# Attention scores as full-height matrix products: high and low query halves stacked in the array's rows

## The chip, the cores and the metric

One core of one Trainium2 chip runs the whole kernel. The metric is device time in microseconds (us), the median of several executions. TensorE (PE) multiplies matrices; its weight loads are a row of their own in the profile (PEld). VectorE (DVE), ScalarE (ACT) and GpSimd (POOL) do element-wise work, each in the order in which its instructions were written; SyncE (SP) starts transfers.

## The reference, cut to what matters

One layer of causal attention with a linear position penalty, 256 tokens, width 1024, 16 heads of 64. The sequence is one block long, so the block selection falls away.

```
h = rms_norm(x, norm_g)                       # 256 x 1024
q, k, v, gate = split(h @ w_in, 4)            # w_in 1024 x 4096
s = q_h @ k_h.T / 8 - slope_h * (t_q - t_k)   # per head, t_k <= t_q
o_h = softmax(s) @ v_h
out = rms_norm(x + (o * silu(gate)) @ w_out, final_g)
```

## The kernel before

Every product is made to nearly full float32 precision from pieces in the format fp32r: an operand is split into a high part (a copy that is rounded to fp32r, made by ACT) and a low part (the rest, a subtraction, made by DVE). A product is then high x high, plus high x low, plus low x high: three matmuls.

The weights arrive in 40 pieces of 128 x 1024 numbers. Each is split by `split_hi` (ACT, the copies of line 118) and `split_lo` (DVE, line 252); four pieces can be split ahead of their use. The projections run in the order of `PARTS`: v 0, q 0, k 0, g 0, q 1, k 1, g 1, q 2, k 2, q 3, k 3, v 1, g 2, g 3. A part of q, k or g gives four heads, that is two pairs of heads; `j` counts the parts and `p` the pairs. The output projection follows, with the 8 pairs as its 8 steps, and the last steps (pairs 4 to 7) stand at its end. The final norm and the stores come after it.

When a part of q or k is done, `fiber_evac` scales it into a tile `z` (DVE, line 512), copies it to the high part (ACT, line 118), and subtracts (DVE, line 524). The two heads of a pair lie in the two halves of the 128 partitions. `scores` then multiplies them for two pairs (four heads) at once, four times in the kernel: each matmul uses the 64 rows of one head, and the two heads of a pair stand next to each other in the program and use different halves of the array. There are 20 such matmuls in a block (line 354). For queries 128 to 255 (`m` = 1) there are three products per head; for queries 0 to 127 (`m` = 0) there are two, of which the first computes high and low keys side by side, and DVE adds these two parts later (line 387). `fiber_pair` makes the softmax: score plus bias with its minimum (lines 387 and 390), exponential (ACT), reciprocal (line 400), normalisation (line 410 on DVE or a copy on ACT, line 407 to 411), transposes (line 111), split of the probabilities (ACT and line 434), product with v, the gate (lines 468 to 474) and the split of the result into `oh` (ACT) and `ol` (line 479).

The order on each engine is written out by the program itself: `Plan` keeps a clock for PE, ACT, DVE and POOL with a cost for each instruction, and "fibers" (one for each evacuation and each pair) are woken when PE's clock passes the time at which their operands should be there. `at_q` and `at_k` hold the time at which a pair's operands are ready; `scores` wakes at the latest of them. `fill` places weight splits when their due time comes near. A normalisation goes to ACT if the plan has ACT more than 800 ns behind DVE's clock, otherwise to DVE:

```
if plan.t["act"] + NORM < plan.t["dve"]:
    d = max(d, act(o, o, AF.Copy, c1 - c0, d_ri, False, scale=ri[:, cc:cc + 1]))
else:
    nc.vector.tensor_scalar(o, o, ri[:, cc:cc + 1], None, op0=ALU.mult)
```

`SWITCH` is a cost of 100 ns that the plan adds before and after a score block. At the start POOL makes 16 bias tiles (`make_bias`, line 221), then the two powers of the norm (line 566).

Of the kernel before, what the change touches and what calls it, by code (L numbers as in the profile page):

```python
# [13 lines left out]
P = 128  # L14
# [43 lines left out]
COLD = 6800.0  # L58
WARM_END = 9000.0
NL = 4  # L60
SWITCH = 100.0


class Plan:
# [18 lines left out]
def f32(ap):  # L83
    return ap.bitcast(F32)
# [3 lines left out]
def trunk(ctx: ExitStack, tc, laid, fin_g, out):  # L88
# [7 lines left out]
    sp = ctx.enter_context(tc.tile_pool(name="sp", bufs=NPR))  # L96
    ptp = ctx.enter_context(tc.tile_pool(name="ptp", bufs=NPT))
    qp = ctx.enter_context(tc.tile_pool(name="qp", bufs=NKB))
    khp = ctx.enter_context(tc.tile_pool(name="khp", bufs=NKB))
    zp = ctx.enter_context(tc.tile_pool(name="zp", bufs=2))  # L100
    csp = ctx.enter_context(tc.tile_pool(name="csp", bufs=2))
    ogp = ctx.enter_context(tc.tile_pool(name="ogp", bufs=2))
# [112 lines left out]
    rows = const.tile([P, S], F32, name="rows")  # L215
    rows8 = const.tile([P, S], F32, name="rows8")
    rowsh = const.tile([P, S], F32, name="rowsh")

    def make_bias(h):
        slope = -(2.0 ** (-8.0 * (h + 1) / H))  # L220
# [104 lines left out]
    def scores(p):  # L325


        while not all(u in at_k and u in at_q for u in (p, p + 1)):
            yield poll()
        yield max(t[u] for t in (at_k, at_q) for u in (p, p + 1))  # L330
        while stage["s"] < p:
            yield poll()
        while True:
            b0 = take(keep[0] + 3)
            if b0 is not None:
                break
            yield poll()
        both = [b0] + [take_now() for _ in range(3)]
        plan.pe += SWITCH
        for u in (p, p + 1):  # L340
            of_pair[u] = both[2 * (u - p):2 * (u - p) + 2], {}
        for m, c in ((1, slice(0, S)), (0, slice(S, S + P))):
            for u in (p, p + 1):
                bs, at_s = of_pair[u]
                (qh, ql), kt = (qs[u][:, 0], qs[u][:, 1]), ks[u]
                n = c.stop - c.start

                terms = ((qh, (0, 1)), (ql, (0,))) if m == 0 else ((qh, (0,)), (qh, (1,)), (ql, (0,)))
                for jj, (q, ts) in enumerate(terms):
                    for a in range(2):  # L350
                        rr = slice(a * DH, (a + 1) * DH)
                        o = bs[a]["t"][:, c.start:c.start + n * len(ts)]
                        o = o.rearrange("p (t n) -> p t n", n=n)
                        nc.tensor.matmul(o, q[rr, m * P:(m + 1) * P], kt[rr, ts[0]:ts[-1] + 1, 0:n],  # L354
                                         start=jj == 0, stop=jj == len(terms) - 1, skip_group_check=True)
                    at_s[m] = plan.mm(n * len(ts))
        plan.pe += SWITCH
        stage["s"] = p + 2
        yield 0

# [127 lines left out]
    def fiber_evac(kind, j, f, b, r):  # L488
        ps = b["t"]
        if kind == "v":  # L490
            hs = slice(j * H // 2, (j + 1) * H // 2)
            ps = ps.rearrange("p (h n) -> p h n", n=DH)
            while not rstd_at:
                yield poll()
            yield max(r, rstd_at[-1]) - 200
            e = act(vv[f][:, hs, 0, :], ps, AF.Copy, CW, max(r, rstd_at[-1]), True, scale=rstd[f])
            yield e - 200
            nc.vector.scalar_tensor_tensor(vv[f][:, hs, 1, :], ps, rstd[f], f32(vv[f][:, hs, 0, :]), op0=ALU.mult, op1=ALU.subtract)
            d = dve(CW, e, extra=62)
            give(b, d)  # L500
            at_v[j] = max(d, at_v.get(j, 0))
            nv[j] += 1
            return
        while not have_rows:
            yield poll()
        yield max(r, have_rows[0]) - 200

        pairs = slice(2 * j, 2 * j + 2)
        ps = ps.rearrange("p (f n) -> p f n", f=2)
        z = zp.tile([P, 2, S], F32, name="z")  # L510
        rb = {"q": rows8, "k": rows, "g": rowsh}[kind].unsqueeze(1).to_broadcast([P, 2, S])
        nc.vector.tensor_mul(z, ps, rb)
        d = dve(2 * S, max(r, have_rows[0]))
        give(b, d)
        if kind != "g":
            while stage["s"] < 2 * (j - NKB + 1):
                yield poll()
        yield d - 100
        if kind != "g":
            pool = qp if kind == "q" else khp  # L520
            both = pool.tile([P, 2, 2, S], F32R, name=kind)
            e = act(both[:, 0], z, AF.Copy, 2 * S, d, False)
            yield e - 100
            nc.vector.tensor_sub(both[:, 1], z, f32(both[:, 0]))
            d = dve(2 * S, e)
            for a in range(2):
                (qs if kind == "q" else ks)[2 * j + a] = both[:, :, a]
                (at_q if kind == "q" else at_k)[2 * j + a] = d
        else:
            e = act(sg[:, pairs, :], z, AF.Tanh, 2 * S, d, False)  # L530
            yield e - 100
            nc.vector.scalar_tensor_tensor(sg[:, pairs, :], sg[:, pairs, :], 1.0, z, op0=ALU.add, op1=ALU.mult)
            d = dve(2 * S, e)
            at_g[2 * j] = at_g[2 * j + 1] = d

    with tc.manual_schedule():
# [48 lines left out]

        for h in range(H):
            make_bias(h)
        warm_to(3480.0)
        acc = banks[4:6]
        for b in acc:  # L590
# [231 lines left out]
```

## Time and profile before

| | |
|---|---|
| median of 3 runs | 143.28 us (143.06 to 143.43) |
| the profiled execution | 143.68 us |
| its span in the trace | 141.9 us |
| mean granted TensorE clock in the span | 0.994 of full speed |
| PE busy | 135.1 us, 95% |
| DVE busy | 122.9 us, 87% |
| ACT busy | 94.4 us, 67% |
| POOL busy | 13.8 us, 10% |

The span is the part of the execution between the first and the last instruction; 1.78 us lie around it. Busy time is the time in which an engine runs at least one instruction. Two consecutive instructions of one engine overlap in part, so the distance between two starts, and not the duration of one, says how much of the engine's time an instruction takes.

### The profile page before, as it was taken

The page shows a single profiled execution, that of the slowest core. Times are in us where ns is not written, and L with a number is a line of the kernel's source. Part 1 is how long each engine was busy: PE and PEld are TensorE (multiplying, and loading weights), DVE is VectorE, ACT ScalarE, POOL GpSimd, SP SyncE. Part 2 cuts the span into 40 slices and gives each one's busy share as a digit, 9 for nine tenths or more (in the row PEclk, how much of TensorE's full clock was granted, in tenths as well). Part 3 has the DMA queues.
Part 4 walks back from the last instruction along what each step waited for, and adds up shares of the span by engine and source line. Part 5 has one row for each costly group of instructions (what it writes and reads, how often), then busy time and mean ns, then how long its engine had stood idle before and what let it go on. Part 6 is the DMA issues. An engine that isn't in the chain of part 4 may idle for free.

```text
span 141.9 us, 2687 instructions
## 1 busy us (share of the span) xinstructions
PE 135.1 (95%) x977; PEld 124.6 (88%) x977; DVE 122.9 (87%) x286; ACT 94.4 (67%) x198; POOL 13.8 (10%) x29
## 2 busy tenths in 40 slices
PE   7999999999999999999999999999999999999930
PEld 5688899999999999999999997778999988888830
DVE  0989579988989999989989999997999999994970
ACT  3498989665878674877772993769959755812340
POOL 7992130000000000000000000000000000000210
PEclk9999999999999999999999999999999999999997
DMA  4999998788204734244445704675055735000034
GB/s 166 321 396 406 404 393 292 241 260 281 106 0 148 216 113 158 109 145 155 159 141 170 258 18 148 200 247 151 0 172 177 245 118 182 0 0 0 0 148 150
DMA packets 8077, 24.81 MB, mean 175 GB/s; under 512 B 896, under 2 KB 1280, under 8 KB 8064
## 3 DMA queue, kind: packets, MB, share of 16 engines
q1 hardware_dynamic: 7632, 23.73, 48.3%
q10 hardware_dynamic: 432, 0.92, 1.7%
q8 instruction: 7, 0.11, 0.3%
q14 instruction: 6, 0.05, 0.1%
HBM read 23.60 MB, written 1.05 MB: 174 GB/s over the span
## 4 chain that ended last, share of the span: by engine, by line
PE 91%; issue 3%; DVE 2%; POOL 1%; ACT 1%; POOLq 1%
PE bank L107 81%; PE bank L111 4%; PE bank L354 4%; PE bank L543 2%; DVE x L756 1%; POOL fr L770 1%; DVE bias L760 1%; ACT bias L777 1%; POOLq L818 1%; DVE bias L765 0%; DVE oh L208 0%; DVE fms L732 0%; DVE eps_t L212 0%; DVE fms L760 0%
## 5 line engine op out<-in xcount | busy, mean ns | idle before, releaser
L107 PE MATMUL bank<-xl,whi 128*128 128x256 f32 x192 | 55.2, 288 | 0.0
L107 PE MATMUL bank<-xh,wlo 128*128 128x256 f32 x192 | 55.0, 287 | 0.0
L107 PE MATMUL bank<-xh,whi 128*128 128x256 f32 x192 | 55.0, 287 | 0.0
L252 DVE TENSOR_TENSOR wlo<-w,whi 128x1024 fp32r<-128x1024 f32 (+1 forms) x43 | 48.6, 1136 | 4.6 <-ACT whi L118 4.5
L118 ACT ACTIVATE whi<-w 128x1024 fp32r<-128x1024 f32 (+1 forms) x43 | 41.5, 976 | 13.2 <-PE bank L107 5.9
L107 PEld LDWEIGHTS bank<-xl,whi 128*128 128x128 f32 x192 | 36.2, 188 | 0.2
L107 PEld LDWEIGHTS bank<-xh,whi 128*128 128x128 f32 x192 | 36.2, 188 | 0.2
L107 PEld LDWEIGHTS bank<-xh,wlo 128*128 128x128 f32 x192 | 36.2, 188 | 0.0
L118 ACT ACTIVATE pr<-st,mx 128x256 f32<-128x256 f32 (+1 forms) x32 | 14.2, 447 | 1.8 <-DVE mx L390 1.6
L770 POOL TENSOR_TENSOR fr<-fms,mhalf 128x1 f32<-128x1 f32 x2 | 1.6, 799 | 114.7 <-DVE fms L760 114.7
L107 PE MATMUL bank<-whi,oh 128*128 128x512 f32 (+1 forms) x35 | 12.3, 352 | 0.0
L107 PE MATMUL bank<-wlo,oh 128*128 128x512 f32 (+1 forms) x35 | 12.3, 351 | 0.0
L107 PE MATMUL bank<-whi,ol 128*128 128x512 f32 (+1 forms) x35 | 12.3, 351 | 0.0
L107 PE MATMUL bank<-whi,xh 128*128 128x512 f32 x32 | 12.3, 425 | 0.0
L111 PE MATMUL bank<-ident,pr 128*128 128x128 f32 x48 | 12.0, 272 | 0.0
L107 PE MATMUL bank<-whi,xl 128*128 128x512 f32 x32 | 11.9, 415 | 0.0
L107 PE MATMUL bank<-wlo,xh 128*128 128x512 f32 x32 | 11.9, 414 | 0.0
L118 ACT ACTIVATE pt<-bank 128x384 fp32r<-128x384 f32 x16 | 7.8, 489 | 3.2 <-PE bank L111 3.1
L107 PE MATMUL bank<-pt,vv 128*128 128x256 f32 x48 | 9.8, 281 | 0.0
L434 DVE TENSOR_TENSOR pt<-bank,pt 128x384 fp32r<-128x384 f32 x16 | 8.7, 551 | 0.7 <-ACT pt L118 0.6
L221 POOL TENSOR_SCALAR bias<-dist 128x256 f32<-128x256 f32 x16 | 8.8, 551 | 1.0
L107 PEld LDWEIGHTS bank<-pt,vv 128*128 128x128 f32 x48 | 8.1, 189 | 0.2
(80 smaller groups left out, 195.4 us busy)
## 6 DMA issues: line engine op xcount, KB each, us to landing
w<-in_laid SPq DMA_DIRECT2D x36, 512.0 KB, 3.5
w<-in_laid SPq DMA_DIRECT2D x7, 256.0 KB, 5.5
x<-in_laid SPq DMA_DIRECT2D x2, 512.0 KB, 6.9
head<-in_laid SPq DMA_DIRECT2D x3, 256.0 KB, 5.7
gf<-in_fin_g ACTq DMA_DIRECT2D x1, 512.0 KB, 5.5
out<-bias SPq DMA_DIRECT2D x2, 256.0 KB, 2.0
out<-bias SPq DMA_DIRECT2D x1, 320.0 KB, 2.3
w<-in_laid ACTq DMA_DIRECT2D x1, 256.0 KB, 2.9
```

The lines of the kernel that those rows point to most:

```text
L107: nc.tensor.matmul(o, a, b, start=start, stop=stop, skip_group_check=True)
L111: nc.tensor.transpose(o, a, ident)
L118: nc.scalar.activation(o, i, fn, scale=scale, **kw)
L221: nc.gpsimd.tensor_scalar(bias[:, h, :], dist, slope, 0.0, op0=ALU.mult, op1=ALU.add)
L252: nc.vector.tensor_sub(wlo[i][:, c], w32[i][:, c], f32(whi[i][:, c]))
L354: nc.tensor.matmul(o, q[rr, m * P:(m + 1) * P], kt[rr, ts[0]:ts[-1] + 1, 0:n], start=jj == 0, stop=jj == len(terms) - 1, skip_group_check= ...
L434: nc.vector.tensor_sub(lo, pv, f32(hi))
L543: nc.tensor.matmul(banks[7]["t"].rearrange("p (a n) -> p a n", n=P), zr, zr.unsqueeze(1).to_broadcast([P, CW // P, P]), start=True, stop=True)
L756: nc.vector.tensor_add(y[:, c], o, y[:, c])
L760: nc.vector.tensor_tensor_reduce(sq[:, :c1 - c0], y[:, c], y[:, c], scale=1.0 / D, scalar=ms[:, u - 1:u], op0=ALU.mult, op1=ALU.add, accum ...
L770: nc.gpsimd.tensor_tensor(r, ms[:, ns - 1:ns], mhalf, op=ALU.pow)
L777: nc.scalar.activation(z[:, 0:CW], z[:, 0:CW], AF.Copy, scale=r)
```

## The change

The scores use the whole height of the array. For each head, a query tile holds the head's high queries in the head's own 64 partitions and its low queries in the other 64. The key tile holds the high keys in both halves and, as its second part, the low keys in the head's own half with zeros beside them. One product with the high keys thus gives high x high plus low x high, and one with the low keys gives high x low. A block of two pairs has 12 matmuls of 256 columns and 128 rows: two per head for the late queries, and one per head for the early ones (high and low keys side by side as before). The key tiles are two fixed tiles that are used in turn; their zeros are written once, by POOL, in four memsets after the bias tiles. To lay out these tiles, the evacuation works on one head of each pair at a time, 64 partitions wide: for q two copies and two subtractions instead of one of each, for k four copies and two subtractions. The plan counts the new instructions and drops `SWITCH`.

```diff
+    kt = [const.tile([P, 2, 2, 2, S], F32R, name=f"kt{i}") for i in range(NKB)]
+    def clear(i):
+        for a in range(2):
+            o = kt[i][(1 - a) * DH:(2 - a) * DH, a, :, 1]
+            nc.gpsimd.memset(f32(o), 0.0)
...
-        plan.pe += SWITCH
-        for m, c in ((1, slice(0, S)), (0, slice(S, S + P))):
-            for u in (p, p + 1):
-                bs, at_s = of_pair[u]
-                (qh, ql), kt = (qs[u][:, 0], qs[u][:, 1]), ks[u]
-                n = c.stop - c.start
-                terms = ((qh, (0, 1)), (ql, (0,))) if m == 0 else ((qh, (0,)), (qh, (1,)), (ql, (0,)))
-                for jj, (q, ts) in enumerate(terms):
-                    for a in range(2):
-                        rr = slice(a * DH, (a + 1) * DH)
-                        o = bs[a]["t"][:, c.start:c.start + n * len(ts)]
-                        o = o.rearrange("p (t n) -> p t n", n=n)
-                        nc.tensor.matmul(o, q[rr, m * P:(m + 1) * P], kt[rr, ts[0]:ts[-1] + 1, 0:n], ...)
-                    at_s[m] = plan.mm(n * len(ts))
-        plan.pe += SWITCH
+        for u in (p, p + 1):
+            bs, at_s = of_pair[u] = both[2 * (u - p):2 * (u - p) + 2], {}
+            for m in (1, 0):
+                for a in range(2):
+                    q, k = qs[u][:, a, m * P:(m + 1) * P], ks[u][:, a]
+                    if m:
+                        for t in range(2):
+                            nc.tensor.matmul(bs[a]["t"][:, 0:S], q, k[:, t], start=t == 0, stop=t == 1, ...)
+                            at_s[m] = plan.mm(S)
+                    else:
+                        o = bs[a]["t"][:, S:S + 2 * P].rearrange("p (t n) -> p t n", n=P)
+                        nc.tensor.matmul(o, q, k[:, :, 0:P], start=True, stop=True, ...)
+                        at_s[m] = plan.mm(S)
...
-            pool = qp if kind == "q" else khp
-            both = pool.tile([P, 2, 2, S], F32R, name=kind)
-            e = act(both[:, 0], z, AF.Copy, 2 * S, d, False)
-            yield e - 100
-            nc.vector.tensor_sub(both[:, 1], z, f32(both[:, 0]))
-            d = dve(2 * S, e)
+            both = qp.tile([P, 2, 2, S], F32R, name="q") if kind == "q" else kt[j % NKB]
+            for a in range(2):
+                own, other = slice(a * DH, (a + 1) * DH), slice((1 - a) * DH, (2 - a) * DH)
+                hi = both[own, a] if kind == "q" else both[own, a, :, 0]
+                lo = both[other, a] if kind == "q" else both[own, a, :, 1]
+                e = act(hi, z[own], AF.Copy, 2 * S, d, False)
+                if kind == "k":
+                    act(both[other, a, :, 0], z[own], AF.Copy, 2 * S, d, False)
+                yield e - 100
+                nc.vector.tensor_sub(lo, z[own], f32(hi))
+                d1 = dve(2 * S, e)
+            d1 = max(d1, plan.t["act"] + 145.0)
...
+        for i in range(NKB):
+            clear(i)
```

## Rows read from the trace of the kernel before

**Rows 1.** The page: the chain that ended last, shares of the span by line.

```profile
PE bank L107 81%; PE bank L111 4%; PE bank L354 4%; PE bank L543 2%; DVE x L756 1%; POOL fr L770 1%; DVE bias L760 1%; ACT bias L777 1%; POOLq L818 1%; DVE bias L765 0%; DVE oh L208 0%; DVE fms L732 0%; DVE eps_t L212 0%; DVE fms L760 0%
```

**Rows 2.** Busy time by stretch; the order of engines is PE, PEld, DVE, ACT.

```profile
41.40:127.70 86.30, 86.30 (x662) 80.85 (x661) 82.72 (x195) 61.08 (x131) 0.00 (x0) 1.00 0.42 141
```

**Rows 3.** Timeline of PE at the first score block: start, length, instruction.

```profile
31.54 0.28 PE L107 MATMUL bank<-xh,wlo 128*128 128x256 f32 x1
...
31.89 0.28 PE L107 MATMUL bank<-xh,wlo 128*128 128x256 f32 x1
32.10 1.38 PE L354 MATMUL bank<-k,q 64*128 64x256 f32 x20
...
33.64 0.28 PE L107 MATMUL bank<-xl,whi 128*128 128x256 f32 x1
```

**Rows 4.** Groups by line: loads of weights beside the projection matmuls.

```profile
L107 PEld LDWEIGHTS bank<-xh,whi 128*128 128x128 f32 x192 | 36.2, 188 | 0.2
```

**Rows 5.** Timelines of DVE and of ACT in the evacuation of q 0.

```profile
26.16 0.69 DVE L524 TENSOR_TENSOR q<-z,q 128x512 fp32r<-128x512 f32 x1
26.77 2.35 DVE L252 TENSOR_TENSOR wlo<-w,whi 128x1024 fp32r<-128x1024 f32 x2
25.48 0.65 ACT L118 ACTIVATE q<-z 128x512 fp32r<-128x512 f32 x1
26.00 1.08 ACT L118 ACTIVATE whi<-w 128x1024 fp32r<-128x1024 f32 x1
```

**Rows 6.** Instructions by tile, 64 and 128 partitions: shortest/median/longest ns, first and last start.

```profile
L468 DVE TENSOR_TENSOR og<-bank,cs x16: 406/416/419, 47.4 to 123.5; 64x256 f32<-64x256 f32 x16
L474 DVE TENSOR_TENSOR og<-og,head x8: 414/418/427, 50.0 to 124.3; 128x256 f32<-128x256 f32 x8
```

**Rows 7.** Timeline of DVE, its idle times over 0.2 us from 30 us to 128 us.

```profile
32.52 1.23 DVE L252 TENSOR_TENSOR wlo<-w,whi 128x1024 fp32r<-128x1024 f32 x1 [1.02 <-ACT whi L118]
41.37 1.23 DVE L252 TENSOR_TENSOR wlo<-w,whi 128x1024 fp32r<-128x1024 f32 x1 [0.57 <-ACT whi L118]
62.69 1.23 DVE L252 TENSOR_TENSOR wlo<-w,whi 128x1024 fp32r<-128x1024 f32 x1 [0.57 <-ACT whi L118]
71.45 0.42 DVE L468 TENSOR_TENSOR og<-bank,cs 64x256 f32<-64x256 f32 x1 [0.43 <-ACT cs L118]
96.26 0.56 DVE L434 TENSOR_TENSOR pt<-bank,pt 128x384 fp32r<-128x384 f32 x1 [0.64 <-ACT pt L118]
98.36 0.75 DVE L498 SCALAR_TENSOR_TENSOR vv<-bank,rstd,vv 128x512 fp32r<-128x512 f32 x1 [0.21 <-ACT vv L118]
```

**Rows 8.** DVE's last instructions ahead of the final norm, and the matmuls that read them.

```profile
124.98 1.22 DVE L252 TENSOR_TENSOR wlo<-w,whi 128x1024 fp32r<-128x1024 f32 x1
127.25 0.42 DVE L479 TENSOR_TENSOR ol<-og,oh 128x256 fp32r<-128x256 f32 x1
127.73 0.39 PE L107 MATMUL bank<-wlo,oh 128*128 128x512 f32 x1
129.37 0.39 PE L107 MATMUL bank<-xh,ol 128*128 128x512 f32 x1
```

**Rows 9.** Timeline of DVE: normalisations after the last evacuation of k.

```profile
87.69 0.69 DVE L524 TENSOR_TENSOR k<-z,k 128x512 fp32r<-128x512 f32 x1
88.50 0.81 DVE L410 TENSOR_SCALAR pr<-pr,ri 128x256 f32<-128x256 f32 x3
```

**Rows 10.** Timeline of PE: the last score block.

```profile
89.49 1.39 PE L354 MATMUL bank<-k,q 64*128 64x256 f32 x20
```

**Rows 11.** Timeline of POOL at the start.

```profile
2.04 9.67 POOL L221 TENSOR_SCALAR bias<-dist 128x256 f32<-128x256 f32 x16
16.45 0.56 POOL L566 TENSOR_TENSOR rstd<-ms,mhalf 128x1 f32<-128x1 f32 x1 [4.75 <-DVE ms L563]
```

**Rows 12.** Timeline of DVE at the start: a low part beside POOL's work, and a later idle time.

```profile
10.56 0.88 DVE L252 TENSOR_TENSOR wlo<-w,whi 128x512 fp32r<-128x512 f32 x1
18.53 1.23 DVE L252 TENSOR_TENSOR wlo<-w,whi 128x1024 fp32r<-128x1024 f32 x1 [2.16 <-ACT whi L118]
```

More of the change, by code (lines that the diff above doesn't have):

```diff
@@ L60 @@
 NL = 4
-SWITCH = 100.0
 class Plan:
@@ L98, in trunk @@
     qp = ctx.enter_context(tc.tile_pool(name="qp", bufs=NKB))
-    khp = ctx.enter_context(tc.tile_pool(name="khp", bufs=NKB))
     zp = ctx.enter_context(tc.tile_pool(name="zp", bufs=2))
@@ L338, in scores @@
         both = [b0] + [take_now() for _ in range(3)]
-        plan.pe += SWITCH
         for u in (p, p + 1):
-            of_pair[u] = both[2 * (u - p):2 * (u - p) + 2], {}
-        for m, c in ((1, slice(0, S)), (0, slice(S, S + P))):
-            for u in (p, p + 1):
-                bs, at_s = of_pair[u]
-                (qh, ql), kt = (qs[u][:, 0], qs[u][:, 1]), ks[u]
-                n = c.stop - c.start
-                terms = ((qh, (0, 1)), (ql, (0,))) if m == 0 else ((qh, (0,)), (qh, (1,)), (ql, (0,)))
-                for jj, (q, ts) in enumerate(terms):
-                    for a in range(2):
-                        rr = slice(a * DH, (a + 1) * DH)
-                        o = bs[a]["t"][:, c.start:c.start + n * len(ts)]
-                        o = o.rearrange("p (t n) -> p t n", n=n)
-                        nc.tensor.matmul(o, q[rr, m * P:(m + 1) * P], kt[rr, ts[0]:ts[-1] + 1, 0:n],
-                                         start=jj == 0, stop=jj == len(terms) - 1, skip_group_check=True)
-                    at_s[m] = plan.mm(n * len(ts))
-        plan.pe += SWITCH
+            bs, at_s = of_pair[u] = both[2 * (u - p):2 * (u - p) + 2], {}
[4 more added lines that the diff above has]
+                        for t in range(2):
+                            nc.tensor.matmul(bs[a]["t"][:, 0:S], q, k[:, t], start=t == 0, stop=t == 1,
+                                             skip_group_check=True)
+                            at_s[m] = plan.mm(S)
+                    else:
+                        o = bs[a]["t"][:, S:S + 2 * P].rearrange("p (t n) -> p t n", n=P)
+                        nc.tensor.matmul(o, q, k[:, :, 0:P], start=True, stop=True, skip_group_check=True)
+                        at_s[m] = plan.mm(S)
         stage["s"] = p + 2
@@ L519, in fiber_evac @@
         if kind != "g":
-            pool = qp if kind == "q" else khp
-            both = pool.tile([P, 2, 2, S], F32R, name=kind)
-            e = act(both[:, 0], z, AF.Copy, 2 * S, d, False)
-            yield e - 100
-            nc.vector.tensor_sub(both[:, 1], z, f32(both[:, 0]))
-            d = dve(2 * S, e)
-            for a in range(2):
-                (qs if kind == "q" else ks)[2 * j + a] = both[:, :, a]
-                (at_q if kind == "q" else at_k)[2 * j + a] = d
+            both = qp.tile([P, 2, 2, S], F32R, name="q") if kind == "q" else kt[j % NKB]
+            for a in range(2):
+                own, other = slice(a * DH, (a + 1) * DH), slice((1 - a) * DH, (2 - a) * DH)
[9 more added lines that the diff above has]
+            for a in range(2):
+                if kind == "q":
+                    qs[2 * j + a], at_q[2 * j + a] = both[:, :, a], d1
+                else:
+                    ks[2 * j + a], at_k[2 * j + a] = both[:, :, a], d1
         else:
```

## Prediction

> **What bounds the kernel now.** I read the chain that ended last first. It is TensorE nearly alone: the projection and value matmuls of line 107 hold 81% of the span and the score matmuls of line 354 another 4%, with engines other than TensorE only at its two ends [rows 1]. The table by stretches says the same for the middle: from 41.4 to 127.7 us TensorE is busy for the whole 86.30 us. It says a second thing, though: VectorE is busy for 82.72 of these 86.3 us, ScalarE for only 61.08 [rows 2]. So I listed VectorE's idle times. Up to the first two pairs' softmax there are 1.02 and 0.57 us; after 41.4 us only four are longer than 0.2 us: 0.57, 0.43, 0.64 and 0.21, in all 1.85 us [rows 7]. What else is missing from 86.3 is the small step (about 0.04 us) ahead of an instruction that reads the one before it. VectorE is therefore a second, nearly full engine, and the question is how far ahead of TensorE it runs where the two meet last. That is in the output projection: the low part of weight piece 38 ends at 124.98 + 1.22 = 126.20 us and its matmul starts at 127.73, a lead of 1.53 us; the low part of the last pair's result ends at 127.25 + 0.42 = 127.67 and its matmul starts at 129.37, a lead of 1.70 us [rows 8]. After that nothing stands before TensorE but its own work. TensorE is the bound, and VectorE is 1.5 us from being it.
>
> **TensorE's part.** The last projection matmul before the first block starts at 31.89 us; the second one after the block starts at 33.64, that is 1.75 us for two plain matmuls and the block [rows 3]. Plain ones follow each other by (31.89 - 31.54)/3 = 0.117 us [rows 3]. The block so costs 1.75 - 2 x 0.117 = 1.52 us. Its 20 matmuls run as pairs in the two halves of the array, ten slots, 1.17 us if all took the full 0.117; the rest, about 0.35 us, is the change to half-height products and back (the bubble ahead of the first and the slow first matmul behind). The new block is 12 plain matmuls of 128 rows and 256 columns: 12 x 0.117 = 1.41 us, without a change. Per block 0.11 us are saved, in four blocks 0.4 us, all of it on the path if TensorE stays the bound. This is a gain of 0.3%, which is all that the change has to give.
>
> A rule of the Trainium skill speaks against this. Every one of the 192 projection matmuls of one kind has a weight load of 188 ns of its own, and yet such matmuls follow each other by 0.117 us [rows 3, 4]: the load is hidden behind the matmul before. The page "TensorE: Matmul & The Clock Gate" (Part 3, The mechanism) says that a load overlaps with running matmuls only when its row group differs; half-height pairs have two row groups, full-height products share all of theirs. By that rule the new block would pay load and matmul in turn; the trace disagrees for the very shape that the change uses.
>
> **VectorE's part.** For each part of q and of k there are now two subtractions of 64 x 512 in place of one of 128 x 512. No row shows 64 x 512, but 64 partitions take no less than 128: 416 ns for 64 x 256 against 418 ns for 128 x 256 [rows 6]. So each new one costs what one costs now, by the distance of starts 26.77 - 26.16 = 0.61 us [rows 5]. There are eight (four parts of q, four of k): 4.9 us. Those of q 0 and k 0 (1.2 us) fall before 41.4 us, where idle times of 1.02 and 0.57 us follow [rows 7]; the first of these lies behind a weight copy that ScalarE could not start earlier, so I cost them at nothing. If that cover is gone they add 1.2 us. The other six, 6 x 0.61 = 3.66 us, fall into the full stretch. Of its four idle times three (0.43, 0.64, 0.21) wait for ScalarE copying what TensorE made, and shrink when VectorE is late: 1.28 us. The one at 62.69 us waits for a weight copy that stands behind a normalisation on ScalarE, which itself waits for VectorE's reciprocal, and would move along; I leave it out. VectorE is then late by 3.66 - 1.28 = 2.38 us at its last instructions (from 1.81 with all idle times used to 3.66 with none). The smallest lead there is 1.53 us [rows 8], so TensorE waits until 2.38 - 1.53 = 0.85 us after the old time. TensorE's saved 0.4 us doesn't come off this: it only arrives earlier and waits longer.
>
> **What can shift this sum.** The plan assigns each of the 32 normalisations to VectorE or ScalarE by its two clocks, and the change adds to both. A normalisation of 128 x 256 takes about 0.81/3 = 0.27 us of VectorE [rows 9]. If seven of them change sides, in either direction, VectorE gains or loses 1.9 us. The change loads ScalarE more (below), which speaks for moves to VectorE; the fuller clock of VectorE speaks for the opposite. I take none, and keep 1.9 us on both sides for the range.
>
> **ScalarE's part.** One copy more for each part of q and three more for each of k: 16 copies of 0.52 us (starts 25.48 and 26.00) [rows 5], 8.3 us. In the full stretch ScalarE has 25 us without work [rows 2]; I cost them at nothing. If this cover fails it is where copies stand in front of weight splits and exponentials, and their price is at most the three extra copies of one part of k, 1.6 us, at one place.
>
> **The way to the scores.** For k the last subtraction now waits for the third copy, 2 x 0.52 = 1.04 us later than today. In the last block the subtraction ends at 87.69 + 0.69 = 88.38 and the block starts at 89.49 [rows 9, 10], a lead of 1.1 us, which is just used up. The plan knows the new time and puts the block behind more projection work, so I cost it at nothing; without that cover TensorE waits in each block for what VectorE and ScalarE are late beyond this lead. Queued behind the waiting block on TensorE are all the projections.
>
> **POOL's part.** Four memsets stand between the bias tiles and the powers of the norm. No row shows this shape; a bias tile of 128 x 256 takes 9.67/16 = 0.60 us [rows 11], and twice its columns without an input lie between nothing and 1.2 us, so all four between 0 and 4.8 us. POOL idles for 4.75 us before the first power [rows 11]. I take half, 2.4 us, and no cost; at the upper end the power starts 0.05 us late. While POOL works, a low part of 128 x 512 on VectorE takes 0.88 us, against 0.69 us for a subtraction of that size later [rows 5, 12]. For 4.8 us this could add 1 us to VectorE ahead of 18.5 us, where it idles for 2.16 us [rows 12]. No cost.
>
> **The sum.** The profiled execution took 143.68 us; +0.85 gives 144.5. The median of the runs is 0.40 us lower, and I carry the difference over: 143.28 + 0.85 = 144.1 us.
>
> **Rivals.** (1) *VectorE keeps up, TensorE stays the bound.* Place: the same two matmuls in the output projection. If VectorE's lateness there is under the lead of 1.53 us less the 0.4 us that TensorE gains, 1.1 us, nothing is lost and the time is 143.28 - 0.4 = 142.9 us. That needs 1.3 us less than I reckon, five normalisations on ScalarE, or a third of the remaining work placed into idle times. For it: the plan does rebalance, and its due times for weights stay. Against it: six subtractions fall into an engine with 1.85 us of room. (2) *TensorE waits at the score blocks.* VectorE is late by 2.4 us by the last block and the chain to it is 1.04 us longer; the lead is 1.1 us. If the plan's order doesn't make room, TensorE stands for up to 2.3 us there and, with its own gain, ends about 1.9 us late: 145.2 us. For it: the lead is short in this block already. Against it: the plan moves the block by its own estimate of the same chain. (3) *Full-height products don't hide their loads*, so that the change doesn't do what it says: 12 x (0.188 + 0.117) = 3.66 us for a block instead of 1.52, 4 x 2.14 = 8.6 us more, 151.8 us. Against it speak all rows of the projections. This is the skill's rule above. (4) *The new order happens to be better elsewhere*, by more than the 0.4 us: TensorE is without a gap in the table, so there is almost nothing to win.
>
> **How the numbers follow.** Forecast (VectorE late at the output projection) 0.47; rival 1, 0.36; rival 2, 0.13; rival 3, 0.01; rival 4, 0.03. A measurement of this kernel can tell about 0.3%, 0.43 us, from no change. The forecast's own range is 143.4 (lateness 1.81, some normalisations on ScalarE) to 145.4 (no idle time used, 3.66 - 1.53 = 2.13); about 0.08 of its 0.47 lies within 0.43 us. Rival 1 sits at -0.41, on the edge: 0.14 of it counts as faster, 0.22 as the same. So faster 0.14 + 0.03 = 0.17; same 0.22 + 0.08 = 0.30; slower 0.39 + 0.13 + 0.01 = 0.53. The range goes from 142.7 (rival 1 with the scatter of the runs, 0.2 us) to 145.6 (the forecast's top with rival 2); normalisations moving to VectorE in number (up to 1.9 us more) and rival 3 are left out.
>
> **What would show it.** In the profile after: a score block of 12 matmuls at 0.117 us, with no slow first matmul before or behind it (TensorE's part). Eight more subtractions at 0.61 us and sixteen more copies at 0.52 us by the starts. VectorE's last low part of the output projection ends 1.8 to 3.7 us later than at 127.67, and TensorE shows a wait of about 1 us on VectorE among its last matmuls, which it has nowhere now. Rival 1 shows no such wait and the same chain of TensorE, 0.4 us shorter; rival 2 shows a wait of TensorE ahead of the score blocks. The prediction is wrong if VectorE's idle times after 41 us stay as long as they are with eight more instructions in it (then it was not full), or if the normalisations change sides in number.

## The result and the profile after

The changed kernel takes 152.27 us (median of 4 runs, 151.87 to 152.67) where the kernel before took 143.20 beside it: a ratio of 1.0623, 95% interval 1.0592 to 1.0655, 9 us slower. I had forecast 144.1 us, and a range up to 145.6. The direction was right, the size was off by a factor of ten. Times and ratios here and below leave out the few executions that ran more than 1.5% slower than the fastest of the same kernel.

The first part of the page of the changed kernel, busy time and the chain that ended last:

```profile
PE 137.0 (91%) x945; PEld 125.5 (84%) x945; DVE 129.7 (86%) x293; ACT 104.7 (70%) x215; POOL 15.7 (10%) x33
...
DVE 52%; PE 25%; ACT 10%; issue 7%; DMA 2%; POOL 1%; POOLq 0%; ACTq 0%; DVEq 0%
PE bank L105 24%; DVE wlo L259 16%; DVE st L393 6%; ACT whi L116 4%; DVE z L515 4%; DVE og L471 4%; DVE pt L437 3%; DVE q L532 3%; DVE og L473 3%; DVE kt L532 2%; DMA w<-in_laid 2%; DVE st L390 2%; ACT kt L116 2%; DVE og L477 2%; DVE ol L482 2%
```

Before, the chain was TensorE's projections, 81% of the span [rows 1]. Now it is VectorE for 52%. What TensorE waits for, from the table of waits (us in total, times, longest; a wait at the program's start is left out):

```profile
PE bank L109 <- DVE mx L393: 2.3, 1, 2.3
PE bank L105 <- DVE ol L482: 2.0, 1, 2.0
PE bank L105 <- ACT oh L116: 1.9, 3, 1.1
```

TensorE, which waited for nobody from 41.4 to 127.7 us [rows 2], now stands for 6.2 us. Its timeline places the waits, all after 109 us; the score blocks have none:

```profile
109.58 0.39 PE L105 MATMUL bank<-wlo,oh 128*128 128x512 f32 x1
112.26 0.48 PE L109 MATMUL bank<-ident,pr 128*128 128x128 f32 x1 [2.29 <-DVE mx L393]
...
126.80 0.40 PE L105 MATMUL bank<-wlo,oh 128*128 128x512 f32 x1
129.18 0.50 PE L105 MATMUL bank<-whi,ol 128*128 128x512 f32 x1 [1.98 <-DVE ol L482]
...
137.06 0.50 PE L105 MATMUL bank<-xh,oh 128*128 128x512 f32 x1 [1.11 <-ACT oh L116]
```

Behind 109.6 us it waits for VectorE's first step of the softmax of the last pairs (`mx`), behind 126.8 us for the results of these pairs. The first wait is not for an operand: the probabilities that the transpose reads were ready at 107.62 + 0.81 = 108.43 us, and the wait ends with a `mx`, behind which the program gives a bank of scores free (`give`). So TensorE waits there for a bank, one of the pieces of memory into which it writes its results (VectorE's timeline):

```profile
107.62 0.81 DVE L413 TENSOR_SCALAR pr<-pr,ri 128x128 f32<-128x128 f32 x3
...
112.12 0.08 DVE L393 DVE_READ_ACCUMULATOR2_ANT mx<- 128x1 f32 x1
```

VectorE's timeline at that end shows why these come one by one (the row after an `ol` is the next pair's gating; the results of pairs 4 to 7 end at 129.1, 131.9, 134.7 and 137.5):

```profile
131.48 0.43 DVE L482 TENSOR_TENSOR ol<-og,oh 128x256 fp32r<-128x256 f32 x1 [0.48 <-ACT oh L116]
131.82 0.41 DVE L471 TENSOR_TENSOR og<-bank,cs 64x256 f32<-64x256 f32 x1
...
133.35 0.43 DVE L477 TENSOR_TENSOR og<-og,head 128x256 f32<-128x256 f32 x1
134.26 0.43 DVE L482 TENSOR_TENSOR ol<-og,oh 128x256 fp32r<-128x256 f32 x1 [0.48 <-ACT oh L116]
```

One pair takes 134.26 - 131.48 = 2.78 us, VectorE and ScalarE in turn, with nothing else left to put into the 0.48 us in which VectorE waits for ScalarE's copy. Before, only the last two of these results were left after 119 us, with weight pieces between them [rows 8]. Something has changed further ahead, too: the score blocks of pairs 4/5 and 6/7 start at 87.97 and 99.92 us, where they stood at 75.79 and 89.49 [rows 10]. TensorE did not wait for them; the plan wrote them 12 and 10 us later, behind more projections (TensorE's timeline, the first two rows of the changed kernel, the third of the kernel before):

```profile
87.97 0.64 PE L354 MATMUL bank<-kt,q 128*128 128x256 f32 x4
...
99.92 0.64 PE L354 MATMUL bank<-kt,q 128*128 128x256 f32 x4
...
75.79 1.39 PE L354 MATMUL bank<-k,q 64*128 64x256 f32 x20
```

The score block itself is what the diff promises (timeline of TensorE, first block):

```profile
32.88 0.28 PE L105 MATMUL bank<-xl,whi 128*128 128x256 f32 x1
33.00 0.64 PE L354 MATMUL bank<-kt,q 128*128 128x256 f32 x4
33.48 0.40 PE L359 MATMUL bank<-kt,q 128*128 128x256 f32 x2
33.72 0.65 PE L354 MATMUL bank<-kt,q 128*128 128x256 f32 x4
34.20 0.40 PE L359 MATMUL bank<-kt,q 128*128 128x256 f32 x2
34.44 0.28 PE L105 MATMUL bank<-xh,wlo 128*128 128x256 f32 x1
```

From 33.00 to 34.44 it is 1.44 us for 12 matmuls, without a bubble at either end, against 1.52 with the bubbles before [rows 3]. The new instructions, from the groups by line (count, then busy us and mean ns):

```profile
L116 ACT ACTIVATE kt<-z 64x512 fp32r<-64x512 f32 x16 | 10.1, 631 | 2.5 <-DVE z L515 2.2
...
L532 DVE TENSOR_TENSOR q<-z,q 64x512 fp32r<-64x512 f32 x8 | 5.5, 686 | 0.4 <-ACT q L116 0.2
L532 DVE TENSOR_TENSOR kt<-z,kt 64x512 fp32r<-64x512 f32 x8 | 5.4, 680 | 0.1
L116 ACT ACTIVATE q<-z 64x512 fp32r<-64x512 f32 x8 | 5.0, 625 | 0.2
...
L224 POOL MEMSET kt<- 64x512 f32 x4 | 2.1, 520 | 0.2
```

The duration of a subtraction with 64 partitions is what it was with 128: 0.69 us [rows 5]. The distance of starts is not: where an instruction follows directly it is 0.70 to 0.72 us, and 0.60 us for the first one of a part of k, against 0.61 before [rows 5].

### The profile page after: what moved, and what is told of

It reads as the page before. It is cut to its first block, busy times and chain, and to the rows that moved or that the text cites. A ratio compares the mean times of both kernels' runs of the same rounds, so it can differ in the third digit from the quotient of the medians.

```text
span 150.1 us, 2657 instructions
## 1 busy us (share of the span) xinstructions
PE 137.0 (91%) x945; PEld 125.5 (84%) x945; DVE 129.7 (86%) x293; ACT 104.7 (70%) x215; POOL 15.7 (10%) x33
## 4 chain that ended last, share of the span: by engine, by line
DVE 52%; PE 25%; ACT 10%; issue 7%; DMA 2%; POOL 1%; POOLq 0%; ACTq 0%; DVEq 0%
PE bank L105 24%; DVE wlo L259 16%; DVE st L393 6%; ACT whi L116 4%; DVE z L515 4%; DVE og L471 4%; DVE pt L437 3%; DVE q L532 3%; DVE og L473 3%; DVE kt L532 2%; DMA w<-in_laid 2%; DVE st L390 2%; ACT kt L116 2%; DVE og L477 2%; DVE ol L482 2%
## 5 line engine op out<-in xcount | busy, mean ns | idle before, releaser
L105 PE MATMUL bank<-whi,ol 128*128 128x512 f32 (+1 forms) x35 | 13.4, 383 | 2.0 <-DVE ol L482 2.0
L109 PE MATMUL bank<-ident,pr 128*128 128x128 f32 x48 | 12.7, 285 | 2.3 <-DVE mx L393 2.3
L105 PE MATMUL bank<-whi,oh 128*128 128x512 f32 (+1 forms) x35 | 13.5, 386 | 0.8 <-ACT oh L116 0.8
L105 PE MATMUL bank<-wlo,oh 128*128 128x512 f32 (+1 forms) x35 | 13.2, 377 | 0.0
L116 ACT ACTIVATE kt<-z 64x512 fp32r<-64x512 f32 x16 | 10.1, 631 | 2.5 <-DVE z L515 2.2
L105 PE MATMUL bank<-wlo,xh 128*128 128x512 f32 x32 | 11.3, 394 | 0.0
L105 PEld LDWEIGHTS bank<-whi,ol 128*128 128x128 f32 x35 | 7.1, 202 | 3.6 <-DVE ol L482 2.7
L116 ACT ACTIVATE pr<-pr,ri 128x128 f32<-128x128 f32 (+1 forms) x8 | 3.4, 429 | 8.7 <-DVE ri L403 8.7
```

Source lines behind the costliest of these rows:

```text
L105: nc.tensor.matmul(o, a, b, start=start, stop=stop, skip_group_check=True)
L109: nc.tensor.transpose(o, a, ident)
L116: nc.scalar.activation(o, i, fn, scale=scale, **kw)
```

## The experiments

Two things changed at once: the work (matmuls, copies, subtractions) and, since the plan is charged with that work, the order in which every engine gets all its instructions. The experiments take these apart. In the texts on record ahead of the runs a theory is one of the explanations that were weighed, with the time that it would give. Ratios are against the kernel before on the same chip, with 95% intervals.

**All the work, in the order of before.** The plan is charged as before; only then are the new instructions put where the old ones stood.

```diff
+        for m in (1, 0):
+            for u in (p, p + 1):
+                for n in ((S, S, S) if m else (S, P)):
+                    of_pair[u][1][m] = plan.mm(n)
...
-                e = act(hi, z[own], AF.Copy, 2 * S, d, False)
+                los.append((lo, z[own], f32(hi)))
+                nc.scalar.activation(hi, z[own], AF.Copy, scale=1.0)
...
+            e = plan.op("act", 92 + 2 * S / 1.2, d)
+            yield e - 100
+            for args in los:
+                nc.vector.tensor_sub(*args)
+            d1 = dve(2 * S, e)
```

> All of the change (whole-array score matmuls, the split evacuation with its 16 more copies and 8 more subtractions, the memsets), but the plan is charged as in the kernel before, so that every engine keeps the order of the kernel before and only the new instructions stand in it. Theory A (the order: the plan answered the new costs by writing the score blocks of pairs 4 to 7 some 10 us later, and the softmax of the last pairs then stands alone at the end): 143.3 to 144.7 us, what the work itself costs. Theory B (the work: VectorE and ScalarE cannot carry it wherever it stands): about 152 us. Theory C (the full-height matmuls are slow): about 152 us.

Measured: 148.24 us, 1.0345 (1.0321 to 1.0369). TensorE waits inside all four score blocks and nowhere behind them. The last block, TensorE and then VectorE:

```profile
92.98 0.28 PE L363 MATMUL bank<-kt,q 128*128 128x256 f32 x1
93.95 0.50 PE L363 MATMUL bank<-kt,q 128*128 128x256 f32 x2 [0.69 <-DVE kt L543]
94.67 0.39 PE L363 MATMUL bank<-kt,q 128*128 128x256 f32 x1 [0.22 <-DVE kt L543]
...
92.08 1.22 DVE L260 TENSOR_TENSOR wlo<-w,whi 128x1024 fp32r<-128x1024 f32 x1
93.22 1.40 DVE L543 TENSOR_TENSOR kt<-z,kt 64x512 fp32r<-64x512 f32 x2
94.64 0.18 DVE L410 RECIPROCAL ri<-rs 128x4 f32<-128x4 f32 x1
```

The block's low-key products wait for the two subtractions, one after the other. The time lies between the theories: the work alone, without any change of order, costs about 4.7 to 4.9 us, which is more than theory A allowed and about half of what B and C did. What is left of the loss has to come with the order.

**Late blocks alone.** The kernel before, with nothing but the score blocks of pairs 4/5 and 6/7 held back to the times on the plan's clock at which the changed kernel writes them:

```diff
+        yield {4: 82960.0, 6: 94020.0}.get(p, plan.pe)
```

> The kernel before with one thing changed: the score blocks of pairs 4/5 and 6/7 are written as late in the plan's time as in the changed kernel (not before 83 and 94 us of the plan's clock). No work is added, matmuls and evacuation are the old ones. Theory A (order): 149 to 152 us. Theory B (work) and theory C (matmuls): 143.2 us, since none of their causes is in it.

Measured: 147.53 us, 1.0287 (1.0261 to 1.0314). The blocks start at 88.67 and 104.12 us, the second one 4 us later than in the changed kernel. TensorE's largest wait is the one that the changed kernel has at its end too (table of waits):

```profile
PE bank L107 <- ACT oh L118: 2.7, 2, 1.7
```

With no work added, late blocks are enough for a loss of 4.1 us, less than the 5.4 us or more that theory A expected. They are one way to lose it; the next runs show that they are not the whole of it.

**The matmuls alone.** Evacuation and order of before; the blocks are 12 full-height matmuls on the old tiles (scores come out summed over two heads).

```diff
+                    q = (qh, ql)[a][:, m * P:(m + 1) * P]
...
+                            nc.tensor.matmul(bs[a]["t"][:, 0:S], q, kt[:, t], start=t == 0, stop=t == 1,
...
+                        nc.tensor.matmul(o, q, kt[:, :, 0:P], start=True, stop=True, skip_group_check=True)
```

> The kernel before with its own evacuation and its own order on every engine, but the score block made of the 12 matmuls of 128 rows on the old tiles (rows of two heads are summed, so the scores are not the reference's; the shapes, counts and the work behind them are those of the change). Theories A and B: 142.8 us, 0.4 us less than before. Theory C (full-height products do not hide their loads): 145 us or more, up to 152.

Measured: 143.21 us against 143.59, 0.998 (0.9958 to 1.0001). This is the whole gain that the change has to give, and it is at the edge of what can be told from none.

**The copies alone, and the subtractions alone.** Both in the order of before with the 12-matmul blocks. The first adds ScalarE's 16 copies and leaves VectorE its one subtraction per part; the second adds VectorE's eight subtractions and leaves ScalarE its one copy (each leaves out the pieces that it does not make).

```diff
+                nc.scalar.activation(both[own, a] if kind == "q" else both[own, a, :, 0], z[own], AF.Copy, scale=1.0)
...
+            if kind == "q":
+                nc.vector.tensor_sub(ol[:, 2 * j:2 * j + 2, :], z, f32(both[:, 0]))
```

> As e1_same_order (all engines in the order of the kernel before, score blocks of 12 matmuls), but with ScalarE's part of the new evacuation alone: two copies for q, four for k; VectorE makes one subtraction of 128 x 512 as before (the low queries and one head's low keys are left out of the scores). Theory V (the 4.7 us of e1_same_order are VectorE's eight subtractions in a full engine): 142.8 to 143.8 us. Theory S (they are ScalarE's copies, which the score block waits for): 145 to 148 us.

```diff
+            hi = both[:, 0] if kind == "q" else both[:, 0, :, 0]
+            nc.scalar.activation(hi, z, AF.Copy, scale=1.0)
...
+                nc.vector.tensor_sub(both[other, a] if kind == "q" else both[own, a, :, 1], z[own], f32(hi[own]))
```

> The counterpart: all engines in the order of the kernel before, score blocks of 12 matmuls, ScalarE makes one copy of 128 x 512 as before, and VectorE the two subtractions of 64 x 512 (some of the high parts are left out of the scores). Theory V: 146 to 148.3 us. Theory S: 142.8 to 144.5 us.

Measured: copies 144.49 us, 1.0072 (1.0044 to 1.0101); subtractions 148.01 us, 1.0321 (1.0263 to 1.0379). Over the matmuls alone (0.998) that is 0.9% or 1.3 us for the copies and 3.4% or 4.9 us for the subtractions; with the intervals, 0.6 to 2.1 us and 3.8 to 6.0 us. Most of the work's cost is VectorE's. The copies fall between the two theories' ranges, the subtractions into that of theory V. The table of waits of the second kernel:

```profile
PE bank L364 <- DVE kt L538: 3.6, 4, 1.2
```

One of these four, at its last block, in TensorE's timeline:

```profile
92.47 0.28 PE L364 MATMUL bank<-kt,qt 128*128 128x256 f32 x1
93.94 0.62 PE L364 MATMUL bank<-kt,qt 128*128 128x256 f32 x3 [1.19 <-DVE kt L538]
```

**The order alone.** The counterpart of the first experiment: the work of before (one copy, one subtraction, 20 half-height matmuls), but the plan is charged with all of the change, so that every engine has the order of the changed kernel.

```diff
-        plan.pe += SWITCH
...
+        for u in (p, p + 1):
+            for m in (1, 0):
+                for _ in range(4 if m else 2):
+                    of_pair[u][1][m] = plan.mm(S)
...
+                if a == 0:
+                    e = act(both[:, 0], z, AF.Copy, 2 * S, d, False)
+                else:
+                    e = plan.op("act", 92 + 2 * S / 1.2, d)
+                if kind == "k":
+                    plan.op("act", 92 + 2 * S / 1.2, d)
...
+                if a == 0:
+                    nc.vector.tensor_sub(both[:, 1], z, f32(both[:, 0]))
+                d1 = dve(2 * S, e)
```

> The kernel before in its work (one copy and one subtraction of the whole tile, the 20 half-height matmuls of a score block), but written in the order of the changed kernel: the plan is charged with all that the change adds, so the score blocks of pairs 4/5 and 6/7 stand about 12 and 10 us later among the projections. Theory (the order by itself costs a good half of the loss, whatever work goes with it): TensorE waits at the end of the program on ol and oh of the last pairs, 146.5 to 148.5 us, ratio 1.022 to 1.036, near e2's 147.5. Rival (the order costs only because VectorE has the extra work to do in it): without that work VectorE gets through the softmax of the last pairs in time, below 145 us, ratio under 1.012, and e2's late blocks were a worse order than the changed kernel's.

Measured: 150.15 us, 1.0496 (1.0441 to 1.0551), more than the theory had allowed. TensorE's waits are those of the changed kernel, in the same places (from 109.60 to 111.61 us, from 124.80 to 127.15, and ahead of the last pieces):

```profile
PE bank L107 <- DVE ol L480: 1.9, 1, 1.9
PE bank L111 <- DVE mx L391: 1.6, 1, 1.6
...
PE bank L107 <- ACT oh L118: 1.0, 1, 1.0
```

The order by itself is worth 7.1 of the 8.9 us. What the work adds in this order is 1.0623 - 1.0496 = 1.3%, 1.8 us (with the two intervals, 0.6 to 3.1 us).

**Another order, with and without the work.** The changed kernel with `SLACK` 0 in place of 1000 (how early the plan splits weights), and the same order with the work of before.

```diff
-SLACK = 1000.0
+SLACK = 0.0
```

> The changed kernel with one constant of its plan changed (weight splits are due 1 us later: SLACK 0 instead of 1000), the same instructions in another order; in the plan's own clock the last matmul is 5.7 us earlier, with the score blocks of pairs 4/5 and 6/7 at 76 and 86 us instead of 83 and 94. Theory A (half of the changed kernel's loss is order): 146 to 149 us. Theory B (the work costs 9 us in whatever order): 151 to 153 us.

> e11 with SLACK 0 in place of 1000: the work of the kernel before (one copy and one subtraction of the whole tile, the 20 half-height matmuls), in the order of e7 on every engine. It is to e7 what e11 is to the changed kernel. If the price of the extra work is what VectorE has no idle time for, it must show here at about its full size, since e7's VectorE had next to no idle time left: e7's 146.2 less 3 to 4.7 us gives 141.5 to 143.5 us (ratio 0.988 to 1.002), that is, an order that costs nothing by itself. If this order too costs something without the work, the time stands at 144.5 to 146 (1.008 to 1.02), and the work costs less than 2 us in it.

Measured: with the work 146.20 us, 1.0201 (1.0143 to 1.026); without it 144.88 us, 1.0112 (1.0077 to 1.0146). The same instructions as in the changed kernel are 6 us faster in another order. The work adds 0.9% or 1.3 us in it, less than the 3 to 4.7 us that I expected if VectorE had no room at all; as the two intervals touch, this run does not tell it from nothing.

**The free banks.** A score block waits in the plan until five banks are free. Without that rule:

```diff
-            b0 = take(keep[0] + 3)
+            b0 = take(0) if len([b for b in banks if not b["busy"]]) > keep[0] + 3 else None
```

> The changed kernel, but a score block no longer waits in the plan until five banks of PSUM are free by the clock; it takes any four that are not reserved. Its third block is then written at 76.9 us of the plan's clock, when its operands are due, and not at 83.0. If that wait for banks is what makes the order bad: 146 to 148 us, as with e7_slack_0. If it is the lateness of the operands and the crowd behind it (the plan's own clock gains only 0.7 us): 151 to 152.3 us.

Measured: 152.32 us, 1.0619 (1.0575 to 1.0662). The third block now starts at 81.68 us, 6 us earlier, and nothing is won. But the block doesn't run through: TensorE stands in it until VectorE's `pt` has read a bank (TensorE's timeline):

```profile
84.11 0.50 PE L354 MATMUL bank<-kt,q 128*128 128x256 f32 x2 [1.55 <-DVE pt L437]
```

So this run shows that dropping the rule alone doesn't help. What an earlier block would be worth with banks at hand it doesn't show, since it trades one wait for another.

**The evacuation's work with the old matmuls, ordered by the plan.**

```diff
+    kx = [const.tile([P, 2, 2, S], F32R, name=f"kx{i}") for i in range(NKB)]
...
+                e = act(both[own, 0], z[own], AF.Copy, 2 * S, d, False)
+                if kind == "k":
+                    act(kx[j % NKB][other, a], z[own], AF.Copy, 2 * S, d, False)
...
+                nc.vector.tensor_sub(both[own, 1], z[own], f32(both[own, 0]))
```

> The kernel before with its old score matmuls and old tiles, plus the work of the new evacuation (two copies and two subtractions of 64 partitions for q, four and two for k, the two further copies of k into a tile that nobody reads), charged to the plan, which orders everything anew. Theory A (order): the plan puts the last score block 7 us of its clock later than before (the third one stays early), so 147 to 152 us. Theory B (work): about 152 us. Theory C: 143.2 us.

Measured: 150.58 us, 1.0526 (1.0473 to 1.0579). Here too the plan orders for the new work; its blocks stand at 74.75 and 96.76 us, one early and one late, and TensorE waits 4.4 us on ScalarE's `oh` of the last pairs. The time is inside theory A's range, but it can't be read as the price of the work.

**Two ways to take the work off VectorE and ScalarE.** Normalisations to POOL where its clock is behind VectorE's (with none to ScalarE, `SLACK` -500 and k's copies reordered); and the pieces carried to their places by 40 DMAs, the evacuation as before.

```diff
+SLACK = -500.0
...
+NORM = 1e9
...
+                elif plan.t["pool"] < plan.t["dve"]:
+                    nc.gpsimd.tensor_scalar(o, o, ri[:, cc:cc + 1], None, op0=ALU.mult)
```

> The changed kernel relieved: a normalisation goes to GpSimd where the plan has that engine ahead of VectorE (none to ScalarE), k's two copies into the other half stand behind the two copies that the subtractions wait for, and weight splits are due 1.5 us later. Theory V (VectorE is full): 143.5 to 146.5 us, as 25 instructions of 0.27 us can leave it. Against it, if GpSimd and VectorE disturb each other by as much as at the start (0.88 us for a subtraction in place of 0.69): 147 to 150 us.

```diff
+                    nc.sync.dma_start(f32(both[own, a, :, 0]), f32(h[own]))
+                    nc.sync.dma_start(f32(both[other, a, :, 0]), f32(h[own]))
```

> The changed kernel's tiles and its 12 matmuls, but the evacuation as in the kernel before (one copy and one subtraction of 128 x 512, written to the not yet used result tiles), and the pieces carried to their places by DMAs of 64 x 512 (four for a part of q, six for one of k), for which the plan adds 1.8 us to the operands' due time. Theory V (the loss comes from VectorE's eight subtractions, directly or through the order that the plan chooses for them): 142.7 to 143.8 us. If the way to the scores is what counts, whoever makes it longer (the DMAs take 2 us or more where the copies took 1): 145 to 148 us, with TensorE waiting at the score blocks.

Measured: 147.61 us, 1.0289 (1.0231 to 1.0346), with only eight normalisations on POOL; and 165.16 us, 1.1531 (1.1495 to 1.1566). The first misses theory V's range; as it changes several things at once, it doesn't say which of them helped or hurt. The second is far above both of its ranges. The page's row of the DMAs of k's high parts (the last number is us to landing):

```profile
kt<-oh SPq DMA_DIRECT2D x16, 128.0 KB, 4.7
```

TensorE stands for these transfers at the score blocks (table of waits):

```profile
PE bank L355 <- DMA kt<-oh: 8.8, 3, 4.0
PE bank L355 <- DMA kt<-ol: 5.1, 4, 2.0
```

No version came out faster than the kernel before by what a measurement can tell.

## Why the prediction was wrong

The rows of busy time by stretch (PE, PEld, DVE, ACT, as in [rows 2]), from 41.40 us to the end of VectorE's last `ol`, settle most of it. The changed kernel:

```profile
41.40:137.47 96.07, 89.89 (x642) 82.88 (x640) 88.07 (x201) 68.75 (x144) 0.00 (x0) 0.98 0.37 127
```

The order alone, in the same view:

```profile
41.40:135.63 94.23, 89.72 (x664) 82.19 (x663) 83.58 (x195) 61.17 (x132) 0.00 (x0) 0.98 0.38 129
```

And the same row of the others, VectorE's column only; "idle" is the stretch less the busy time, and the last column is the start of the first matmul of weight piece `xh` on TensorE:

| order | work | stretch | VectorE busy | idle | TensorE at `xh` | ratio |
|---|---|---|---|---|---|---|
| before | before | 86.27 | 82.72 | 3.55 | 128.90 | 1 |
| before | subtractions, matmuls | 90.74 | 87.52 | 3.22 | 133.37 | 1.0321 |
| before | all | 91.47 | 88.09 | 3.38 | 133.82 | 1.0345 |
| late blocks | before | 91.87 | 83.50 | 8.37 | 132.86 | 1.0287 |
| SLACK 0 | before | 88.61 | 82.89 | 5.72 | 129.60 | 1.0112 |
| SLACK 0 | all | 90.41 | 87.70 | 2.71 | 131.40 | 1.0201 |
| changed | before | 94.23 | 83.58 | 10.65 | 135.22 | 1.0496 |
| changed | all | 96.07 | 88.07 | 8.00 | 137.06 | 1.0623 |

The end of the program follows this stretch: TensorE reaches `xh` 8.16 us later in the changed kernel, and the span is 150.1 - 141.9 = 8.2 us longer. The busy column has two levels, without and with the work, 4.5 to 5.4 us apart. The idle column depends mostly on the order. For the order of before it has to be read with care: where the work is added, VectorE is 0.82 and 1.44 us late at 41.40 us already, and an idle time of 0.57 us that lay just ahead of 41.40 us falls into the stretch. Counted from the same weight split (at 41.37, 42.19 and 42.81 us) the three stretches are 86.30, 89.95 and 90.06 us, with 3.55, 2.65 and 2.78 us idle (the kernel before and the subtractions alone, in the same view):

```profile
41.37:127.67 86.30, 86.30 (x662) 80.86 (x661) 82.75 (x195) 61.11 (x131) 0.00 (x0) 1.00 0.42 141
...
42.19:132.14 89.95, 86.86 (x638) 81.53 (x637) 87.30 (x201) 61.53 (x131) 0.00 (x0) 1.00 0.40 135
```

So in the order of before the idle time takes up 0.9 us or less of some 4.5 us of work, and the rest lengthens the stretch. In the changed order VectorE idles for 10.65 us without the work. Of these, 4.56 us lie between 60 and 88 us, ahead of the late third block, where the kernel before idles for 1.48 us; 1.95 us lie behind 124.8 us, where one pair follows the other. That VectorE lacks score work in the first of these stretches is my reading; the profile names ScalarE's copies and TensorE's results as what it waits for there. The work fills 2.65 of the 10.65 us, and the stretch grows by only 1.84. That is why the two parts, 4.9 us of work in the old order and 7.1 us of order, don't add up to the whole.

**TensorE's part: right.** 1.44 us for a block where I reckoned 1.41, and 0.3 us for the four (0.4). Rival 3 is refuted: the blocks' full-height matmuls, each with a load of its own, start 0.12 us apart. That its 151.8 us lie near the measured 152.27 is chance. The Trainium skill's page "TensorE: Matmul & The Clock Gate" (Part 3, The mechanism) has a load overlap with running matmuls only when its row group differs, and this trace disagrees. The same section names a second way, which the prediction left out: a load into the background weight buffer is also pulled ahead. POOL's memsets took 2.1 us (2.4), and no normalisations changed side in number (VectorE's went from 25 to 24).

**VectorE's part: wrong at every term of 0.85 us.** The kernel with the subtractions alone has the order that I reckoned with. There VectorE's last `ol` ends 132.14 - 127.67 = 4.47 us late, and the two rows from the same weight split show how. "I cost them at nothing" for the two of q 0 and k 0: they leave VectorE 42.19 - 41.37 = 0.82 us late. 3.66 us for the other six: they add 87.30 - 82.75 = 4.55 us. My price of 0.61 us was too low, because two subtractions of 64 partitions take 1.31 to 1.44 us by the starts in the place of one of 0.61 (in the first experiment 94.64 - 93.22 = 1.42 us), so that the added one costs 0.70 to 0.83. 1.28 us of idle time used up: it was 3.55 - 2.65 = 0.90 us, although the three idle times that I named are gone. Together 0.82 + 4.55 - 0.90 = 4.47 us. That the 4.9 us of this experiment are also 8 x 0.61 is chance.

The last term is "the smallest lead there is 1.53 us", which I took off: a lead at the end is worth nothing when the engines meet earlier. TensorE reaches `xh` 133.37 - 128.90 = 4.47 us late, just as late as VectorE; the lead of 1.23 us at that place is untouched. TensorE had already stood at the four score blocks, for 3.6 us in all. That is rival 2's mechanism at four blocks, not at the last one alone.

**ScalarE's part: not free.** I cost the copies at nothing. The 16 copies cost 1.3 us by the runs, near the 1.6 that I named as the price without cover. Their distance is larger than I took: in the first experiment the four copies of a part of k start at 91.13, 91.78, 92.44 and 93.09, 0.65 us apart and not 0.52 [rows 5], so that the wait for the third copy is 1.3 us and not 1.04.

**The way to the scores: the step that failed most.** "The plan knows the new time and puts the block behind more projection work, so I cost it at nothing." The first half is what happened, by 12 and 10 us. The second half overlooked that what depends on a block moves with it: softmax, value products, gating and the low parts of four pairs, the last of them 2.8 us apart, with no projection left for TensorE to do meanwhile. I had used this re-ordering as a cover against rival 2, and in [rows 8] reckoned with the old order throughout. TensorE does wait in the output projection on VectorE's last instructions, as the forecast said, but mostly for the order's reason, and 6.2 us in all where I had 0.85. By the sign that I had named myself the prediction is wrong, too: VectorE's idle time after 41 us didn't shrink but went from 3.55 to 8.00 us. Among the rivals the new order was only allowed to be better.

**What stays open.** That the order as a whole costs 7.1 us is shown, and that late blocks alone cost 4.1. Which of the plan's other choices make up the rest is not: the variant without the bank rule has its third block 6 us earlier at the same time, and the one with the old matmuls has it earlier than before and loses 5.3%. Nor is it shown what part the banks have: TensorE's first wait in the changed kernel, and the one inside the early block of the variant without the rule, are both for a bank.

## What to carry to other kernels

Where a planner orders the work, an added instruction has two prices, its time and the order that its cost brings about; they can be measured apart, by doing the work without charging it and by charging it without doing it, and here the second was the larger. Two engines that are both full have no cover for each other: an engine's lead over the other has to be read at every place where they meet, not at the last one. And when a step is moved later, follow what depends on it to the program's end and ask what is left to do beside it.

## What the runs showed of the hardware

In the changed kernel TensorE, after the wait of 2.29 us that ends at 112.26, was granted half its clock, 1.2 GHz, from 112 to 115 us; after the wait of 1.98 us that ends at 129.18 it kept the full one, 2.4 GHz (busy time by stretch; the number after POOL's is the granted clock):

```profile
113.00:114.00 1.00, 1.00 (x6) 1.00 (x5) 1.00 (x2) 0.36 (x3) 0.00 (x0) 0.50 0.00 0
...
129.20:130.00 0.80, 0.80 (x4) 0.71 (x5) 0.73 (x3) 0.00 (x0) 0.00 (x0) 1.00 0.00 0
```

With the order alone it was the other way round, the full clock after a wait of 1.61 us that ends at 111.61, and half of it from about 128.3 us on, after one of 1.95 us that ends at 127.15:

```profile
111.60:113.00 1.40, 1.39 (x11) 1.32 (x12) 1.25 (x4) 1.40 (x4) 0.00 (x0) 1.00 0.00 0
...
129.00:130.00 1.00, 1.00 (x3) 0.60 (x3) 0.55 (x2) 0.97 (x3) 0.00 (x0) 0.50 0.00 0
```

So a wait can be followed by a slow stretch that adds to it, and these four rows don't say when. The kernel before had no wait and no such stretch between 41.4 and 127.7 us [rows 2]. The lower clock doesn't explain what the order costs, though: of the four runs of the order alone the one with a mean granted clock of 0.995 took 151.23 us, and the three with 0.977 to 0.979 took 149.79 to 150.22. In the changed kernel the two runs with 0.986 and 0.987 took 151.87 and 151.96 us, and the two with 0.975 took 152.58 and 152.67.

A normalisation of 128 x 128 took POOL 748 ns by its row (its spans in a profile are rough) against VectorE's 284 in the changed kernel, and with POOL at work VectorE's own took 395 ns (the variant with normalisations on POOL, groups by line):

```profile
L413 POOL TENSOR_SCALAR pr<-pr,ri 128x128 f32<-128x128 f32 x8 | 6.0, 748 | 85.4 <-DVE ri L403 80.1 <-PE bank L105 5.3
...
L416 DVE TENSOR_SCALAR pr<-pr,ri 128x128 f32<-128x128 f32 x8 | 3.2, 395 | 0.0
```
